# A decoder layer on one core: the second part of a long score row in the next score bank, and a different order of the operand splits

## The chip, the cores and the metric

The kernel runs on 1 core of one Trainium2 chip. Its time is the device time of one execution in microseconds; of three runs of the kernel before, the median is 2106.13 us (2105.40 to 2106.62). The profile is of one further execution, which took 2103.59 us. Engines are named as in the profile: PE is TensorE with its weight loads as PEld, DVE is VectorE, ACT is ScalarE, POOL is GpSimd, and SP is the engine that issues nearly all DMAs.

## The reference

One layer of a decoder with two kinds of attention side by side, over 2048 tokens of width 1024 with 16 learned meta tokens ahead of them, in fp32:

```python
xn = rms_norm(h, norm_gain[l])
proj = xn @ w_in[l]
sb_q, sb_k, sb_v, sw_q, sw_k, sw_v, sb_z, sw_z, g_sb, g_sw = jnp.split(proj, offsets, axis=-1)
o_sb = stick_breaking_attention(sb_q, sb_k, sb_v, valid)        # 8 heads of 64, over all earlier tokens
o_sw = sliding_window_sink_attention(rope(sw_q), rope(sw_k), sw_v, attn_sinks[l], valid)
y_sb = (o_sb * jax.nn.silu(sb_z)) @ w_branch_sb[l]
y_sw = (o_sw * jax.nn.silu(sw_z)) @ w_branch_swa[l]
merged = jax.nn.sigmoid(g_sb) * y_sb + jax.nn.sigmoid(g_sw) * y_sw
h = h + merged @ w_out[l]
```

Stick-breaking attention turns a row of scores z into weights through products of 1 - sigmoid(z) over the later keys:

```python
z = jnp.einsum('bqhd,bkhd->bhqk', q[:, q0:end], k[:, :end]) * scale
log_beta = jax.nn.log_sigmoid(z)
log_1m = jnp.where(mask, log_beta - z, 0.0)
rev = lax.cumsum(log_1m, axis=3, reverse=True)
suffix = jnp.concatenate([rev[..., 1:], jnp.zeros_like(rev[..., :1])], axis=-1)
w = jnp.where(mask, jnp.exp(log_beta + suffix), 0.0)
outs.append(jnp.einsum('bhqk,bkhd->bqhd', w, v[:, :end]))
```

## The kernel before

**Precision.** Matrix products run on fp32 operands that are split in two: a high part h (a cast on ACT) and a low part l = t - h (a subtraction on VectorE, or on GpSimd for some weights). A product is three matmuls, h·h, h·l and l·h. `put(hl, k, t)` (L1007) is such a split of 128 x 512 elements: the cast is L1008, the subtraction L1009.

**Order.** The tokens are reversed and cut into four groups of 512; the first half of the kernel works on groups 2 and 3 (`ga`, `gb` in the code), the second half on groups 0 and 1. In each half follow one another: projections woven with the sliding-window attention, projections woven with the stick-breaking attention (`stick`), and in the first half the last gates, in plain form and then by a scheme with seven products in place of eight (`combined`, `gate_pairs`). At the end of the kernel come the output products (`finish`). TensorE's instructions run in the order in which the program writes them (a manual schedule of PE over the whole kernel). For ACT, VectorE, GpSimd and SP a planner sets the order from a simulated timeline, except in blocks with a manual schedule of their own, which keep the written order among their instructions; others can be put between them.

**PSUM.** The eight banks (128 x 512 fp32) belong to four tags of two each: g for projections, z for scores, t for transposes, o for outputs. A tile of a tag gets a bank of the two that the planner finds free, and its first writer waits until the readers of the tile before are done.

**Stick-breaking attention (`stick`).** `weave` lets the projections, main, and the attention, side, take turns on TensorE. For each head h and group g a row step (n, j) takes the queries of block j against 512 keys. `row` (L896) writes the scores with two matmuls (L915; the two halves of the split q), applies a sigmoid on ACT (L918) and runs a scan on VectorE (L923 with the mask, L925 without) that carries on the product from the row before. The last row of a group (`end`) with four key blocks also has the 16 meta keys, 528 columns, more than a bank holds. Such a row comes once for each head and group, 32 times in all, and is done in two parts:

```python
pieces = [("z", 0, w)]
if end and nb == 4:
    pieces = [("z", 0, w // 2), ("o", w // 2, w // 2 + NM)]
    w += NM
banks = [ps(tag) for tag, _, _ in pieces]
```

`lt` row steps later (6 in the first half, 5 in the second) `turn` transposes blocks of the scanned rows on TensorE (L944) into a t bank and splits them (L126 on ACT, L127 on VectorE). `turn_meta` (L951) transposes the meta columns into an o bank (L954) and copies them to `wm` in four parts, by turns on ACT and VectorE (L958). `values` (L960) sums the products of the turned weights with differences of v in an o bank that a head and group holds from its first to its last values (L970); after the last ones, those with `wm`, ACT evicts the bank in four instructions with a bias (L976), and DMAs write it out. So three kinds of tiles share the two o banks in `stick`: the sums of `values`, the turned meta columns, and the second part of the long row.

**The scheme with seven products.** `first_sums` (L1022) makes four differences `firsts` = xh+xl of group gb less those of ga, in the ring of four tiles `xs` (`ring_x`), and three of the four differences `thirds` between halves of gb, in three tiles `tt` (`short`), before `stick` starts. `combined` (L1027) makes four operands of these: t2 and t4 in its generator `steps`, one k of four at each call, t3 from the thirds, and t1 from the firsts. t1 is written over the first half of `xh[gb]`, `xl[gb]` (L1031), which the plain gates still read. In `steps` the generator splits the three thirds into t3 after its last step, then makes the fourth with `step_back` (three VectorE operations, L1017 to L1019) in two more short tiles and splits it. `last` splits the firsts into t1. After the two plain gates the program calls

```python
drain(sums_x[4])
sums_x[5]()
```

that is the rest of `steps`, then `last`, in a manual schedule of VectorE and ACT. `gate_pairs` then runs the products (L1117, matmuls L1121 to L1123) in this order for the first pair: a11·b11, a12·b21, s2·t2, s4·b22, a22·t4, s1·t1, s3·t3, with banks g, z, t in turn; VectorE adds them (L1127) and so frees the banks. `pair_weights` (L1062) loads and splits the weights of a pair (L115, L119) and makes their sums (L1072 to L1088). `sums_ahead` (L1093) loads x for the next half into the `xs` ring, which the firsts hold until t1 is split, and squares it on ACT (L1101).

Of the kernel before, what the change touches and what calls it, by code (L numbers as in the profile page):

```python
# [20 lines left out]
NM = 16  # L21
# [22 lines left out]
def f32(ap):  # L44
    return ap.bitcast(F32)
# [3 lines left out]
def tile_kernel(ctx, tc, x, xt, meta, metat, gain, w_in, w_sb, w_sw, w_out, sinks, fgain,  # L49
# [16 lines left out]
    def ps(tag):  # L66
        return pp.tile([P, 512], F32, tag=tag, name="ps_" + tag, bufs={"g": 2, "z": 2, "t": 2, "o": 2}[tag])
# [319 lines left out]
    def tmp(dt=F32, rows=P):  # L387
        return tp.tile([rows, GT], dt, tag="tmp", name="tmp", bufs=9)
# [461 lines left out]
    def stick(groups, bp):  # L850
# [17 lines left out]
        def load_kv(h, g):  # L868

            p, a = divmod(h, 2)  # L870
            r = slice(64 * a, 64 * a + 64)
            if h not in kt:
                kt[h] = bp.tile([P, KW], F32R, tag="k", name="kt", bufs=2)
            for c in range(g, 4):
                if (h, c) in vc:
                    continue
                c0 = (c - groups[0]) * GT
                cs = slice(c0, c0 + GT + (NM if c == 3 else 0))
                DMA(kt[h][0:64, cs], kd[p][c][0][r])
                DMA(kt[h][64:128, cs], kd[p][c][1][r])  # L880
                v = vc[h, c] = bp.tile([P, 4, P], F32R, tag="v", name="vc", bufs=5)
                DMA(v, vd[p][c][a])

        def load_q(h, g):
            p, a = divmod(h, 2)
            r = slice(64 * a, 64 * a + 64)
            q1 = bp.tile([P, GT], F32R, tag="q1", name="q1", bufs=2)
            q2 = bp.tile([P, GT], F32R, tag="q2", name="q2", bufs=2)
            for t in range(2):
                DMA(q1[64 * t:64 * t + 64], qd[p][g][t][r])  # L890
                DMA(q2[64 * t:64 * t + 64], qd[p][g][1 - t][r])
            return q1, q2
# [3 lines left out]
        def row(h, g, n, j):  # L896

            if n == j == 0:
                load_kv(h, g)
                state[h, g] = {"q": load_q(h, g), "last": {}}  # L900
            st = state[h, g]
            last = st["last"]
            b0 = 4 * (g + n) + j
            nb = min(4, NB - b0)
            end = b0 + nb == NB
            w = nb * P + (NM if end and nb < 4 else 0)
            k0 = (b0 - 4 * groups[0]) * P
            pieces = [("z", 0, w)]
            if end and nb == 4:
                pieces = [("z", 0, w // 2), ("o", w // 2, w // 2 + NM)]  # L910
                w += NM
            banks = [ps(tag) for tag, _, _ in pieces]
            for t, qt in enumerate(st["q"]):
                for z, (_, c, m) in zip(banks, pieces):
                    T.matmul(z[:, :m], lhsT=qt[:, j * P:(j + 1) * P], rhs=kt[h][:, k0 + c:k0 + c + m], start=t == 0, stop=t == 1)  # L915
            r = bp.tile([P, RW], F32, tag="row", name="row", bufs=12)
            for z, (_, c, m) in zip(banks, pieces):
                A.activation(r[:, c:c + m], z[:, :m], AF.Sigmoid, scale=-1.0)  # L918
            if n == 0 and mask is None:
                G.affine_select(out=r[:, :P], in_=r[:, :P], pattern=[[1, P]], compare_op=ALU.is_ge,  # L920
                                fill=1.0, base=-1, channel_multiplier=-1)
            if n == 0 and mask is not None:
                V.tensor_tensor_scan(r[:, :w], r[:, :w], mask[:, :w], 1.0, op0=ALU.mult, op1=ALU.max)  # L923
            else:
                V.tensor_tensor_scan(r[:, :w], r[:, :w], r[:, :w], last[j] if n else 1.0, op0=ALU.mult, op1=ALU.min)  # L925
            last[j] = r[:, w - 1:w]
            rows_of[h, g, n, j] = r
            if end:
                if j == 0:
                    st["mr"] = bp.tile([P, 4, NM], F32, tag="mr", name="mr", bufs=2)  # L930
                G.tensor_copy(st["mr"][:, j], r[:, w - NM:w])  # L931
                if j == 3:
                    m = st["m"] = bp.tile([P, 4, 2, NM], F32R, tag="m", name="m", bufs=2)
                    A.copy(m[:, :, 0], st["mr"])
                    V.tensor_tensor(m[:, :, 1], st["mr"], f32(m[:, :, 0]), op=ALU.subtract)
# [48 lines left out]
        for s in range(n + lt + 3):  # L984
# [3 lines left out]
            t = s - lt  # L988
# [16 lines left out]
    HK = KT // 2  # L1005

    def put(hl, k, t):  # L1007
        A.copy(hl[0][:, k, :], t)  # L1008
        V.tensor_tensor(hl[1][:, k, :], t, f32(hl[0][:, k, :]), op=ALU.subtract)  # L1009

    def part(g, k):
        return f32(xh[g][:, k, :]), f32(xl[g][:, k, :])

    def step_back(t, k, g, k1, g1, e):

        (h0, l0), (h1, l1) = part(g, k), part(g1, k1)
        V.tensor_tensor(t, h0, h1, op=ALU.subtract)  # L1017
        V.tensor_tensor(e, l0, l1, op=ALU.subtract)
        V.tensor_tensor(t, t, e, op=ALU.add)  # L1019
        return t  # L1020
# [6 lines left out]
    def combined(ga, gb, pool, short, firsts, thirds):  # L1027

        t2, t3, t4 = [tuple(pool.tile([P, HK, GT], F32R, tag=f"{n}{s}", name=f"{n}{s}") for s in "hl")
                      for n in ("t2", "t3", "t4")]  # L1030
        t1 = (xh[gb], xl[gb])  # L1031

        def steps():
            rest = lambda: None
            for k, s in enumerate(firsts):
                (h21, l21), (h22, l22) = (part(g, k + HK) for g in (ga, gb))
                u, w = tmp(), tmp()
                V.tensor_tensor(u, h22, s, op=ALU.subtract)
                rest()
                V.tensor_tensor(u, u, l22, op=ALU.add)  # L1040
                A.copy(t2[0][:, k, :], u)
                V.tensor_tensor(w, h21, u, op=ALU.subtract)
                V.tensor_tensor(w, w, l21, op=ALU.add)
                A.copy(t4[0][:, k, :], w)
                V.tensor_tensor(t2[1][:, k, :], u, f32(t2[0][:, k, :]), op=ALU.subtract)

                def rest(k=k, w=w):
                    V.tensor_tensor(t4[1][:, k, :], w, f32(t4[0][:, k, :]), op=ALU.subtract)

                yield  # L1050
            rest()
            for k, t in enumerate(thirds):
                put(t3, k, t)
            for k in range(len(thirds), HK):
                put(t3, k, step_back(short(), k + HK, gb, k, gb, short()))

        def last():
            for k in range(HK):
                put(t1, k, firsts[k])
        return t1, t2, t3, t4, steps(), last  # L1060

    def pair_weights(c, d, pool, out, begin=False):  # L1062
# [282 lines left out]
    for half, groups in enumerate(halves):  # L1345
        gts = [lambda spec=spec: gate(*spec) for spec in specs[half]]
        with tc.tile_pool(name=f"swa{half}", bufs=1, side="left") as sp:
# [40 lines left out]
            else:  # L1388
                for mk, gs_ in ((sw_k, groups), (sw_v, groups), *((f, groups[:1]) for f in q[0])):
                    w, use, _ = mk()  # L1390
# [12 lines left out]
        if half == 0:  # L1403
            tt = mid.enter_context(tc.tile_pool(name="mid", bufs=1, side="left"))
            short = lambda: tt.tile([P, GT], F32, tag="tt", name="tt", bufs=3)
# [13 lines left out]
        if half == 0:  # L1419
            with tc.tile_pool(name="fast", bufs=1, side="left") as bp:  # L1420
                pairs = list(zip(specs[0][-FAST::2], specs[0][-FAST + 1::2]))
                sums_x = combined(*groups, bp, short, *early)
                byhand = ExitStack()
                byhand.enter_context(tc.manual_schedule(engines={mybir.EngineType.DVE}))
                with tc.manual_schedule(engines={mybir.EngineType.Activation}):
                    for n in range(PLAIN):
                        w, use, _ = plain[n]
                        for g in groups:
                            next(sums_x[4])
                            if n + 1 == PLAIN and g == groups[1]:  # L1430
                                drain(first_pair)
                            drain(lagged(col_tile(w, g, use)))
                        if n + 2 < PLAIN:
                            plain.append(gts[rest + n + 2]())
                        elif n + 2 == PLAIN:
                            nxt = []
                            first_pair = pair_weights(pairs[0][0][0], pairs[0][1][0], bp, nxt, True)
                            next(first_pair)
                    drain(sums_x[4])
                    sums_x[5]()  # L1440
                rs = tp.tile([P, 8], F32, tag="rs8", name="rs", bufs=1)
                rs0, rs1 = rs[:, :4], rs[:, 4:]
                gate_pairs(*groups, pairs, bp, sums_x, nxt, byhand.close, sums_ahead(halves[1], rs, short),
                           lambda: prep(halves[1][0], rs0))
                hsplit[0] = False
# [68 lines left out]
```

## Time and profile before

| | us |
|---|---|
| median of the three runs | 2106.13 |
| profiled execution | 2103.59 |
| its span | 2101.5 |
| PE busy | 2079.5 |
| DVE busy | 1474.4 |
| ACT busy | 1073.0 |
| POOL busy | 353.2 |

The span is the time from the first to the last instruction of the profiled execution; the 2.1 us around it belong to its time too. Busy times are sums of what each engine's instructions took. Matmuls overlap one another, and their ends are modelled; where the next matmul follows at once, its start lies before the end of the one ahead, so that the distance between starts is the surer measure. In the list of waits, a line names the engine and the line that waited, then what ended the wait, then the sum of the waits in us, their number and the longest. In the timeline each line has the start and the length in us, the engine, the line of the kernel, the operation, what it writes and reads, and in brackets the idle time of its engine just before and what ended it. "x4" means that four such instructions are drawn together.

The stick-breaking attention of the first half lies between 371 and 590 us of the span, the first pair of the seven-product scheme between 613 and 634 us, and the stick-breaking attention of the second half between 1110 and 1605 us.

### The profile page before, as it was taken

How to read it: one execution, taken by the hardware profiler on the slowest of the kernel's cores; microseconds unless marked ns; L12 is line 12 of the kernel's file. 1: busy time of each engine (PE TensorE's matmuls, PEld its weight loads, DVE VectorE, ACT ScalarE, POOL GpSimd, SP SyncE). 2: the span in 40 equal slices, each digit the busy share in tenths (PEclk: the TensorE clock that was granted, in tenths of full speed). 3: DMA queues.
4: the chain of work that ended last, by engine and by line, in shares of the span. 5: the costliest groups of instructions: out<-in, count | busy, mean ns of one | idle time of the engine just before them, and what ended most of it. 6: DMA issues, size and time to landing. Idle time of an engine off the chain costs nothing.

```text
span 2101.5 us, 31090 instructions
## 1 busy us (share of the span) xinstructions
PE 2079.5 (99%) x10591; PEld 1745.5 (83%) x10591; DVE 1474.4 (70%) x2430; ACT 1073.0 (51%) x2586; POOL 353.2 (17%) x692
## 2 busy tenths in 40 slices
PE   9999999999999999999999999999999999999998
PEld 7888888887888888888888888888888888888887
DVE  7898986877777554878747888878774446564553
ACT  6687774555656334877744555555554202320121
POOL 1234445322000000232310000000000243000000
PEclk9999999999999999999999999999999999999999
DMA  9855645766448674434445443443424996568432
GB/s 338 318 196 183 204 158 190 235 184 200 147 141 320 235 259 155 153 143 169 149 164 164 126 131 121 121 125 97 126 91 149 357 325 205 193 224 306 158 100 90
DMA packets 170094, 391.48 MB, mean 186 GB/s; under 512 B 23728, under 2 KB 28208, under 8 KB 169936
## 3 DMA queue, kind: packets, MB, share of 16 engines
q1 hardware_dynamic: 169648, 389.23, 55.2%
q8 instruction: 84, 1.38, 0.3%
q14 instruction: 74, 0.61, 0.1%
q10 hardware_dynamic: 288, 0.27, 0.0%
HBM read 241.68 MB, written 145.18 MB: 184 GB/s over the span
## 4 chain that ended last, share of the span: by engine, by line
PE 91%; DVE 3%; ACT 2%; DMA 2%; issue 1%; POOL 1%; SPq 0%; ACTq 0%; DVEq 0%; POOLq 0%
PE ps_g L461 39%; PE ps_o L970 6%; PE ps_z L915 5%; PE ps_t L944 5%; PE ps_z L756 3%; PE ps_o L812 2%; PE ps_z L461 2%; PE ps_g L258 1%; PE ps_g L259 1%; PE ps_g L260 1%; PE ps_z L258 1%; PE ps_z L259 1%; PE ps_z L260 1%; PE ps_t L258 1%; PE ps_t L259 1%; PE ps_t L260 1%
## 5 line engine op out<-in xcount | busy, mean ns | idle before, releaser
L461 PE MATMUL ps_g<-xh,wh 128*128 128x512 f32 x1296 | 529.3, 408 | 1.0 <-DVE tmp L677 0.6
L461 PE MATMUL ps_g<-xl,wh 128*128 128x512 f32 x1296 | 507.7, 392 | 0.5 <-DVE xl L1193 0.4
L461 PE MATMUL ps_g<-xh,wl 128*128 128x512 f32 x1296 | 507.6, 392 | 0.0
L925 DVE TENSOR_TENSOR_SCAN row<-row 128x512 f32<-128x512 f32 (+4 forms) x256 | 292.0, 1141 | 80.6 <-ACT row L918 45.5
L461 PEld LDWEIGHTS ps_g<-xh,wl 128*128 128x128 f32 x1296 | 243.4, 188 | 54.3 <-DVE wl L1241 0.4
L461 PEld LDWEIGHTS ps_g<-xh,wh 128*128 128x128 f32 x1296 | 244.2, 188 | 40.3 <-ACT xh L1192 1.3
L461 PEld LDWEIGHTS ps_g<-xl,wh 128*128 128x128 f32 x1296 | 244.7, 189 | 38.5 <-DVE xl L1193 1.6
L918 ACT ACTIVATE row<-ps_z 128x512 f32<-128x512 f32 (+2 forms) x320 | 165.5, 518 | 175.0 <-PE ps_z L915 170.3
L126 ACT ACTIVATE wth<-ps_t 128x512 fp32r<-128x512 f32 (+1 forms) x320 | 171.5, 536 | 67.1 <-PE ps_t L944 64.0
L127 DVE SCALAR_TENSOR_TENSOR wtl<-ps_t,wth 128x512 fp32r<-128x512 f32 (+1 forms) x320 | 189.7, 593 | 22.2 <-ACT wth L126 20.6
L915 PE MATMUL ps_z<-kt,q 128*128 128x512 f32 (+4 forms) x640 | 179.0, 354 | 0.0
L944 PE MATMUL ps_t<-ident,row 128*128 128x128 f32 x1088 | 171.0, 272 | 1.3 <-DVE wtl L127 1.3
L944 PEld LDWEIGHTS ps_t<-ident,row 128*128 128x128 f32 x1088 | 135.3, 140 | 34.1 <-DVE wtl L127 1.9
L915 PEld LDWEIGHTS ps_z<-kt,q 128*128 128x128 f32 x640 | 117.6, 188 | 22.3 <-ACT row L918 0.3
L970 PE MATMUL ps_o<-wth,vc 128*128 128x512 f32 (+1 forms) x320 | 131.8, 412 | 1.1 <-ACT tmp L976 1.1
L970 PE MATMUL ps_o<-wtl,vc 128*128 128x512 f32 (+1 forms) x320 | 116.3, 364 | 0.0
L764 ACT ACTIVATE sc<-sc,nm 128x129 f32<-128x129 f32 x256 | 100.0, 393 | 30.0 <-DVE nm L762 29.0
L931 POOL COPY mr<-row 128x16 f32<-128x16 f32 x128 | 27.9, 220 | 452.6 <-DVE row L925 410.4
L612 ACT ACTIVATE tmp<-ps_g 128x512 f32<-128x512 f32 x84 | 50.3, 599 | 86.6 <-PE ps_g L461 80.1
L117 POOL TENSOR_SCALAR wh<-raw 128x1024 fp32r<-128x1024 f32 (+1 forms) x47 | 53.5, 1138 | 224.6 <-PE ps_g L461 103.9
L123 POOL TENSOR_TENSOR wl<-raw,wh 128x256 fp32r<-128x256 f32 x96 | 86.4, 928 | 2.0
L297 ACT CAST ringl<-gt 128x512 fp32r<-128x512 f32 x32 | 19.9, 622 | 128.6 <-DVE gt L295 127.7
(444 smaller groups left out, 4177.8 us busy)
## 6 DMA issues: line engine op xcount, KB each, us to landing
wh<-h_in_w_in SPq DMA_DIRECT2D x66, 512.0 KB, 3.9
wl<-l_in_w_in SPq DMA_DIRECT2D x66, 512.0 KB, 5.0
h_in_w_in<-wh SPq DMA_DIRECT2D x50, 512.0 KB, 3.5
l_in_w_in<-wl SPq DMA_DIRECT2D x50, 512.0 KB, 4.0
raw<-in_w_in SPq DMA_DIRECT2D x49, 512.0 KB, 5.2
q<-qd SPq DMA_DIRECT2D x128, 128.0 KB, 3.1
vc<-vd SPq DMA_DIRECT2D x48, 256.0 KB, 2.9
kd<-tmp SPq DMA_DIRECT2D x32, 256.0 KB, 3.4
```

The source lines that it names most:

```text
L123: G.tensor_tensor(l[:, c], src[:, c], f32(h[:, c]), op=ALU.subtract)
L126: A.activation(h, acc, AF.Copy, scale=scale)
L127: V.scalar_tensor_tensor(l, acc, scale, f32(h), op0=ALU.mult, op1=ALU.subtract)
L258: T.matmul(acc, lhsT=wh[:, k, :], rhs=h, start=k == 0, stop=False)
L259: T.matmul(acc, lhsT=wh[:, k, :], rhs=l, start=False, stop=False)
L461: T.matmul(acc, lhsT=a[:, k, :], rhs=b[:, k, :], start=k == i == 0, stop=k == KT - 1 and i == 2)
L764: A.activation(sc[:, hh, :], sc[:, hh, :], AF.Exp, bias=nm[:, hh:hh + 1], accum_out=den[:, hh:hh + 1])
L915: T.matmul(z[:, :m], lhsT=qt[:, j * P:(j + 1) * P], rhs=kt[h][:, k0 + c:k0 + c + m], start=t == 0, stop=t == 1)
L918: A.activation(r[:, c:c + m], z[:, :m], AF.Sigmoid, scale=-1.0)
L925: V.tensor_tensor_scan(r[:, :w], r[:, :w], r[:, :w], last[j] if n else 1.0, op0=ALU.mult, op1=ALU.min)
L944: T.transpose(tr[:, j * P:(j + 1) * P], rows_of[h, g, n - (j > i), j][:, k0:k0 + P], ident)
L970: T.matmul(o[:, :n], lhsT=v, rhs=r, start=first and r is wh, stop=last)
```

## The change

There are two edits. In `row` the second part of the long row takes a z bank, as the first part does. In `combined` the splits of the thirds move from the end of `steps` to the end of `last`, behind the splits of t1, and the fourth third is made at the start of `last` (it reads the part of gb that t1 overwrites), in tiles of the `tmp` ring of nine in place of short ones.

```diff
@@ row
             if end and nb == 4:
-                pieces = [("z", 0, w // 2), ("o", w // 2, w // 2 + NM)]
+                pieces = [("z", 0, w // 2), ("z", w // 2, w // 2 + NM)]
                 w += NM
@@ combined
                 yield
             rest()
-            for k, t in enumerate(thirds):
-                put(t3, k, t)
-            for k in range(len(thirds), HK):
-                put(t3, k, step_back(short(), k + HK, gb, k, gb, short()))
 
         def last():
+            more = [step_back(tmp(), k + HK, gb, k, gb, tmp()) for k in range(len(thirds), HK)]
             for k in range(HK):
                 put(t1, k, firsts[k])
+            for k, t in enumerate(thirds + more):
+                put(t3, k, t)
```

## The prediction

> **What bounds the kernel now.** I read the page first, then the list of waits, then the timeline at each place where TensorE waits.
>
> ```profile
> span 2101.5 us, 31090 instructions
> ...
> PE 2079.5 (99%) x10591; PEld 1745.5 (83%) x10591; DVE 1474.4 (70%) x2430; ACT 1073.0 (51%) x2586; POOL 353.2 (17%) x692
> ```
>
> TensorE is busy 2079.5 of 2101.5 us. Only the other 22.0 us, and slow starts hidden in busy time, can be won without taking matmuls away; the change takes none away. The list of waits (engine, tile and line; what ended the wait; us in total, times, longest) says where they are. These rows touch the change:
>
> ```profile
> PE ps_o L915 <- DVE wm L958: 4.7, 4, 1.6
> PE ps_o L915 <- ACT tmp L976: 2.6, 3, 1.1
> ...
> PE ps_o L970 <- ACT tmp L976: 1.1, 2, 0.6
> ...
> PE ps_t L1121 <- ACT xh L1008: 1.2, 1, 1.2
> PE ps_z L1121 <- DVE tmp L1127: 0.6, 1, 0.6
> ...
> PE ps_t L1122 <- DVE xl L1009: 0.3, 1, 0.3
> ```
>
> The second part of the long row (ps_o, L915) waits seven times, 7.3 us together, for a bank of the output ring. The first t1 product (L1121, L1122) waits 1.5 us for its operands. Both lie in the first half of the sequence: the seven between 409 and 574 us, the product at 628 us.
>
> **The row's second part: what it removes.** Here is the timeline (start, length, engine, instruction; the bracket is idle time of its engine and what ended it) at an undisturbed row, at the first of the seven and at the last.
>
> ```profile
> 391.87 0.28 PE L915 MATMUL ps_z<-kt,q 128*128 128x256 f32 x1
> 391.98 0.29 PE L915 MATMUL ps_o<-kt,q 128*128 128x272 f32 x1
> ...
> 409.25 0.28 PE L915 MATMUL ps_z<-kt,q 128*128 128x256 f32 x1
> 410.31 0.36 PE L915 MATMUL ps_o<-kt,q 128*128 128x272 f32 x1 [0.79 <-DVE wm L958]
> 410.88 0.40 ACT L918 ACTIVATE row<-ps_z 128x256 f32<-128x256 f32 x1
> 412.13 0.54 PE L915 MATMUL ps_z<-kt,q 128*128 128x400 f32 x2
> ...
> 572.12 0.28 PE L915 MATMUL ps_z<-kt,q 128*128 128x256 f32 x1
> 573.27 0.26 ACT L958 CAST wm<-ps_o 32x128 fp32r<-32x128 f32 x1 [1.83 <-DVE wm L958]
> 573.55 1.14 ACT L976 ACTIVATE tmp<-ps_o,vf 128x128 f32<-128x128 f32 x4
> 574.00 0.36 PE L915 MATMUL ps_o<-kt,q 128*128 128x272 f32 x1 [1.61 <-DVE wm L958]
> 574.57 0.40 ACT L918 ACTIVATE row<-ps_z 128x256 f32<-128x256 f32 x1
> 575.37 0.39 PE L970 MATMUL ps_o<-wth,vc 128*128 128x512 f32 x1
> 575.83 0.53 PE L915 MATMUL ps_z<-kt,q 128*128 128x400 f32 x2
> ```
>
> Undisturbed, the second part starts 0.11 us after the first, the pitch of 256 columns (so 0.23 us for 512). At 409.25 it starts 1.06 us after, at 572.12 1.88 us after: 0.95 and 1.77 us lost. At such a place one output bank still holds the finished output of the head (evicted by L976, 1.14 us), the other the turned meta columns (copied out by ACT and VectorE in turn, L958). By the same subtraction the seven lose 0.95, 1.29, 0.95, 1.65, 1.28, 0.60 and 1.77, together **8.5 us**. Counting starts gives more than the idle 7.3, because a matmul that follows directly starts before the end drawn for the one ahead. The Trainium skill's page "Perfetto Trace Analysis", section "Identifying the Most-Contended Engine", says that matmul busy time misleads because matmuls are pipelined; by idle time alone my terms would come to 9.9 instead of 12.1 us.
>
> The row also takes the bank that the next values want; twice that costs TensorE a wait in the middle of a head:
>
> ```profile
> 446.36 0.38 PE L944 MATMUL ps_t<-ident,row 128*128 128x128 f32 x2
> 447.34 0.50 PE L970 MATMUL ps_o<-wth,vc 128*128 128x512 f32 x1 [0.60 <-ACT tmp L976]
> ```
>
> Two transposes, 256 columns, take 0.11 us; here 0.98 us pass, so 0.87 us are lost for 0.60 us of idle time. For both (1.1 us idle) that makes 1.1 + 2 x 0.27 = **1.6 us**. With the row gone from the ring a bank that was emptied steps earlier is free, so I count all of it (bounds 0 and 1.6).
>
> **What it adds.** Matmuls (256 and 272 columns) and sigmoids stay; no DMA is added. The row now holds both score banks. So its second part waits for the sigmoid of the row before, the next row for sigmoid 1, the one after that for sigmoid 2. Behind a waiting score matmul stands everything on TensorE, and so the transposes, the values and the gate products. In all 32 places I compared the row's start with the end of the sigmoid before it: it has ended, in the closest three of the second half at the very moment (bounds 0 to 0.2 us each; I take 0.3 us for the three). The new wait of the next row has slack too; the tightest of the second half is
>
> ```profile
> 1185.65 0.38 ACT L918 ACTIVATE row<-ps_z 128x256 f32<-128x256 f32 x1
> 1186.60 0.52 PE L915 MATMUL ps_z<-kt,q 128*128 128x400 f32 x2
> ```
>
> sigmoid 1 ends at 1186.03, 0.57 us before. At the seven places the stall itself was the cover. Take it out at 572: the next row would come at 575.83 - 1.77 = 574.06, but sigmoid 1 ends at 574.97, behind L976; and the next values (575.37) would come at 573.60, while L976 ends at 574.69. So about 1.1 us stays. At 409 the next row would come at 411.18 and sigmoid 1 ends at 411.28. Done so for all seven, with the values in L976's bank, 2.5 us stays. Bounds: 0, if the planner, which sets ACT's order anew, puts the sigmoids ahead of L976; 4.1, if the values also get the bank of the slow meta copies wherever that is later. I take 2.5, since ACT's order in the trace is the nearest row. This edit: 8.5 + 1.6 - 2.5 - 0.3 = **7.3 us** (bounds 8.5 - 4.1 - 0.6 = 3.8, and 10.1).
>
> That the other engines follow a faster TensorE is read from the stretch of these rows (length, then busy time and count per engine):
>
> ```profile
> 380.00:590.00 210.00, 200.84 (x1120) 168.73 (x1119) 165.77 (x254) 125.52 (x327) 40.69 (x90) 1.00 0.57 177
> ```
>
> VectorE, the fullest, has 44 us to spare, ACT 84. Clock 1.00.
>
> **The order of the splits.** The timeline at the t1 product:
>
> ```profile
> 613.34 0.39 PE L461 MATMUL ps_g<-xh,wl 128*128 128x512 f32 x1
> ...
> 620.01 1.65 ACT L1008 CAST t3h<-tt 128x512 fp32r<-128x512 f32 x3
> 620.69 0.68 DVE L1048 TENSOR_TENSOR t4l<-tmp,t4h 128x512 fp32r<-128x512 f32 x1
> ...
> 624.30 2.35 DVE L119 TENSOR_TENSOR wl<-raw,wh 128x1024 fp32r<-128x1024 f32 x2
> ...
> 626.94 0.39 PE L1123 MATMUL ps_z<-t4h,wl 128*128 128x512 f32 x1
> 627.29 0.62 ACT L1008 CAST t3h<-tt 128x512 fp32r<-128x512 f32 x1 [1.92 <-DVE tt L1019]
> 627.81 2.18 ACT L1008 CAST xh<-xs 128x512 fp32r<-128x512 f32 x4
> 628.48 0.50 PE L1121 MATMUL ps_t<-xh,sh 128*128 128x512 f32 x1 [1.15 <-ACT xh L1008]
> 628.55 2.49 DVE L1009 TENSOR_TENSOR xl<-xs,xh 128x512 fp32r<-128x512 f32 x4
> 629.29 0.50 PE L1122 MATMUL ps_t<-xl,sh 128*128 128x512 f32 x1 [0.30 <-DVE xl L1009]
> 629.62 0.40 PE L1123 MATMUL ps_t<-xh,sl 128*128 128x512 f32 x1
> ```
>
> At 0.23 us a matmul the product would start at 627.17. It starts 1.31 us late, its second matmul another 0.58, its third 0.10: **2.0 us**. Its inputs xh, xl are written last, after four t3 splits, of which the fourth waits for its sum, which waits behind 2.35 us of weight splits. After the edit ACT can cast xh from 620.0 on (the last reader of the old xh is the matmul at 613.34): four end by 622.2. VectorE does the moved sum (three operations of 0.62) from 621.3 to 623.2, then xl in 2.49: 625.7, or 628.0 if the weight splits go first. The last is wanted at 627.17 + 3 x 0.68 + 0.23 = 629.4. The t3 splits then end by 630.5 at the latest, wanted from 630.1 (first, ready 0.6 us after xl) to 632.2 (last). So the whole 2.0 us goes. The sum uses two tmp tiles instead of two short ones: no instruction more; should the tiles come late, each operation costs 0.62 of that slack.
>
> What could take it back is the next wait of this stretch, in the chain of waits:
>
> ```profile
> 629.26 3.16 DMA xs<-in_x
> ...
> 649.14 6.43 DMA raw<-in_w_in
> ```
>
> xl frees the tiles into which SP loads x, and behind those loads in SP's queue come the weights of a later pair; their lateness is the 0.6 us at ps_z L1121. With xl 3 to 5 us earlier those loads start earlier too, ahead of a TensorE that gains 2.0 there. I cost it at nothing; bounds: a gain of 0.8 (that wait, by starts), or a loss of the whole 2.0 if the weights keep their time. Edit: **2.0** (0 to 2.8).
>
> **Sum.** 7.3 + 2.0 = 9.3 us of the profiled execution's 2103.59 (2101.5 of span and 2.1 around it), so 2094.3. It lay 2.5 below the median of the runs, 2106.13; against that the forecast is **2096.8**. Bounds of the two edits: 3.8 to 12.9 us, so 2093.2 to 2102.3.
>
> **Rivals.**
> *The waits only move* (chance 0.12): in each head the meta copies and L976 hold up the next values instead of the row, and sigmoid 1 the next row, until all 8.5 us are back. Gain 1.6 + 2.0 - 0.3 = 3.3: 2102.8. For it: at 572 1.1 of 1.77 stays. Against it: at 435 and 518 I find nothing that would.
> *Half of it* (0.12): the lower bound, 3.8, with the pair's weights late: 2102.3; or the second edit alone fails because the planner puts weight splits ahead of xl and the sums too, 2106.13 - 7.3 = 2098.8. I take 2100.5 for the middle.
> *Slower* (0.10): a row that fills the score ring leaves no bank in which the next row can run ahead; from then on ACT's order decides. In the second half nothing is won to pay for it. If ACT put L976 (1.14) and a copy of a turned tile (0.60) ahead of sigmoid 1 in all 16 places there, 1.74 against a mean slack of 1.1 us costs 16 x 0.64 = 10.2; with the seven stalls replaced by equal ones and 2.0 won, 2106.1 + 10.2 - 2.0 = 2114.3. It decides from the point where sigmoid 1 starts over 1.1 us later than now. The Trainium skill's "Perfetto Trace Analysis", section "Matmuls", says that independent matmul groups should rotate through different banks so that an evacuation overlaps the next group; by that the row should not take the ring's two. Against it:
>
> ```profile
> ACT row L918 <- PE ps_z L915: 170.3, 238, 1.2
> ```
>
> of 320 such sigmoids 238 found ACT waiting for the score itself: the ring is mostly emptied at once.
> *That the change doesn't do what it says* would be a planner that leaves t1 behind t3; ACT and VectorE have a written order there, so it is inside "half of it".
>
> **How the numbers follow.** Forecast 0.66, half of it 0.12, only moved 0.12, slower 0.10. A measurement here can tell about 0.2%, 4.2 us, so faster is below 2101.9: forecast and the half give 0.78 and "only moved" 0.12 of no change, slower 0.10. The range reaches from the sum of all bounds, 2093.2, less 1 us for places that the planner orders anew, to just past "only moved", 2103.5; the slower rival is left out.
>
> **What would show it.** Right: no wait of L915 in the list, but short ones of L915 or L970 on ps_z or ps_o at 409 to 574, 2 to 3 us together; xh and xl cast ahead of t3 and no wait of L1121 on ps_t; the stretch to the t1 product shorter by 9 us. Wrong: rows of "PE ps_z L915 <- ACT row L918" with over 5 us, above all past 1110 us, or a longer wait of L1121 for L1127.

## The result, and the profile after

| | before | after | |
|---|---|---|---|
| median of the runs taken side by side (4 each), us | 2105.77 | 2093.16 | ratio 0.9941 [0.9924, 0.9958] |
| their range, us | 2104.93 to 2106.62 | 2092.05 to 2094.89 | |
| profiled execution, us | 2103.59 | 2092.70 | |
| its span, us | 2101.5 | 2090.5 | -11.0 |

The changed kernel is 12.6 us faster by the medians and 11.0 by the spans. The two numbers differ because the profile of before is of a quick execution: in the three later sets of runs of that kernel (15, 20 and 9 of them) the lowest times were 2103.97, 2103.63 and 2103.73. The page of the changed kernel:

```profile
span 2090.5 us, 31069 instructions
...
PE 2077.5 (99%) x10591; PEld 1744.9 (83%) x10591; DVE 1473.2 (70%) x2430; ACT 1071.6 (51%) x2586; POOL 350.9 (17%) x692
```

The work is the same (10591 matmuls, busy times within 0.7%); what is missing is idle time, and it is 13.0 us now (2090.5 less 2077.5) where it was 22.0. The list of waits of the changed kernel (what waited, what ended it; us in total, times, longest), its rows that touch the change:

```profile
PE ps_o L970 <- DVE wm L958: 0.5, 2, 0.3
...
PE ps_z L915 <- ACT row L918: 0.3, 1, 0.3
```

The seven waits of the row's second part, the two of the values for L976 and all waits of the t1 product are gone. Three short ones at heads' ends are left in this list, 0.8 us. (In the changed kernel the product's matmuls are L1120 to L1122 and its additions L1126, one line less than before.) The stretch of the long rows, in the view by windows (length, then busy time and count of PE, PEld, DVE, ACT, POOL; clock, DMA share, GB/s):

```profile
380.00:590.00 210.00, 208.36 (x1158) 175.91 (x1157) 171.81 (x266) 129.13 (x337) 41.89 (x90) 1.00 0.58 179
```

In the same 210 us TensorE starts 38 matmuls more, and VectorE and ACT follow with 6.0 and 3.6 us more work each. The clock is 1.00 as before.

**The stages.** One instruction that both kernels have is taken at each border, and the times between their starts are compared. The timeline of before, then that of the changed kernel (start, length, engine, instruction, idle before it), at a long row, the first matmul of the product s4·b22, the first projection that waits for L677, the first matmul of `finish` (L333) and the last DMA:

```profile
382.77 0.36 PE L915 MATMUL ps_z<-kt,q 128*128 128x256 f32 x1
...
624.45 0.39 PE L1121 MATMUL ps_z<-t4h,wh 128*128 128x512 f32 x1
...
848.22 0.50 PE L461 MATMUL ps_g<-xh,wh 128*128 128x512 f32 x1 [0.62 <-DVE tmp L677]
...
1789.46 0.39 PE L333 MATMUL ps_t<-ringr,ringl 128*128 128x512 f32 x1
...
2098.14 0.35 ACTq L370 DMA_DIRECT2D out<-a  x1
```

```profile
382.73 0.49 PE L915 MATMUL ps_z<-kt,q 128*128 128x256 f32 x2
...
615.53 0.39 PE L1120 MATMUL ps_z<-t4h,wh 128*128 128x512 f32 x1
...
836.06 0.50 PE L461 MATMUL ps_g<-xh,wh 128*128 128x512 f32 x1 [0.61 <-DVE tmp L677]
...
1777.32 0.39 PE L333 MATMUL ps_t<-ringr,ringl 128*128 128x512 f32 x1
...
2087.16 0.35 ACTq L370 DMA_DIRECT2D out<-a  x1
```

For each kernel of this study, from the same five starts of its profile (us):

| kernel | row to product | product to projection | to `finish` | `finish` |
|---|---|---|---|---|
| before | 241.68 | 223.77 | 941.24 | 308.68 |
| after | 232.80 | 220.53 | 941.26 | 309.84 |
| after, second profile (e10) | 232.80 | 221.54 | 941.30 | 309.63 |
| e1, first edit only | 232.82 | 222.60 | 941.37 | 311.08 |
| e2, second edit only | 241.58 | 221.36 | 941.21 | 309.66 |
| e9 | 232.80 | 223.11 | 941.29 | 308.89 |
| e5 | 232.86 | 220.99 | 941.29 | 310.02 |
| e3 | 241.37 | 223.11 | 947.22 | 309.04 |
| e4 | 240.18 | 220.48 | 942.50 | 310.30 |
| e8 | 234.56 | 224.67 | 941.19 | 309.69 |
| e7, e11 | 230.63, 230.66 | 220.94, 220.82 | 941.19, 941.30 | 309.46, 309.38 |

The change wins 8.88 us in the first column and 3.24 in the second, nothing in the third, and gives 1.16 back in the last. The first column repeats within 0.1 us for all kernels that have the same code there, the third within 0.2; the second and the last vary by 1 to 2.4 us without an edit there, so a difference of that size in them proves nothing by one profile. Taken together, the twelve profiles say more of the second: with the fourth t3 split ahead of t1 (before, e1, e3, e8, e9) it is 222.60 to 224.67, with that split behind t1 (the other seven) 220.48 to 221.54, on average 2.5 us less.

### The profile page after: what moved, and what is told of

It is laid out like the page before. It is cut to its first block, busy times and chain, and to the rows that moved or that the text cites. A ratio compares the mean times of both kernels' runs of the same rounds, so it can differ in the third digit from the quotient of the medians.

```text
span 2090.5 us, 31069 instructions
## 1 busy us (share of the span) xinstructions
PE 2077.5 (99%) x10591; PEld 1744.9 (83%) x10591; DVE 1473.2 (70%) x2430; ACT 1071.6 (51%) x2586; POOL 350.9 (17%) x692
## 3 DMA queue, kind: packets, MB, share of 16 engines
HBM read 241.68 MB, written 145.18 MB: 185 GB/s over the span
## 4 chain that ended last, share of the span: by engine, by line
PE 93%; DVE 3%; ACT 2%; DMA 1%; issue 1%; POOL 0%; SPq 0%; DVEq 0%; ACTq 0%; POOLq 0%
PE ps_g L461 41%; PE ps_o L970 6%; PE ps_z L915 6%; PE ps_t L944 6%; PE ps_z L756 3%; PE ps_o L812 2%; PE ps_z L461 2%; PE ps_g L260 1%; PE ps_g L258 1%; PE ps_g L259 1%; PE ps_t L790 1%; PE ps_z L260 1%; PE ps_z L258 1%; PE ps_z L259 1%; PE ps_t L260 1%; PE ps_t L259 1%
## 5 line engine op out<-in xcount | busy, mean ns | idle before, releaser
L918 ACT ACTIVATE row<-ps_z 128x512 f32<-128x512 f32 (+4 forms) x352 | 175.0, 508 | 169.5 <-PE ps_z L915 165.6
L915 PE MATMUL ps_z<-kt,q 128*128 128x512 f32 (+4 forms) x704 | 183.6, 349 | 0.4 <-ACT row L918 0.3
L915 PEld LDWEIGHTS ps_z<-kt,q 128*128 128x128 f32 x704 | 124.8, 188 | 25.7 <-ACT row L918 2.7
L970 PE MATMUL ps_o<-wth,vc 128*128 128x512 f32 (+1 forms) x320 | 131.5, 411 | 0.5 <-DVE wm L958 0.5
L970 PE MATMUL ps_o<-wtl,vc 128*128 128x512 f32 (+1 forms) x320 | 116.3, 364 | 0.0
```

The costliest lines, as they stand in the source:

```text
L970: T.matmul(o[:, :n], lhsT=v, rhs=r, start=first and r is wh, stop=last)
```

## The experiments

**Each edit alone.** e1 has only the first line of the diff, e2 only the edit in `combined`.

> Only the first edit: the second part of the long row in a score bank; the splits stay in the old order. Theory (the two edits act in two places and add up): by starts of TensorE the first edit gives back 8.5 (row) + 1.6 (values) less the 1.4 that the changed kernel still loses at its heads' ends, so about 9 us: ratio 0.9957. The late start at the t1 product (2.0) and the wait of a later product for L1127 (0.6 idle, 0.8 by starts) are still there. Rival (the planner's new order of everything after 371 us, and not the banks, brings the gain): the seven waits are gone, but the time is not 8 to 10 us below before, or the losses at the products are gone too.

> Only the second edit: t1 split ahead of t3, the fourth sum in tmp tiles; the row keeps its second part in the output ring. Theory: the 2.0 us at the t1 product go, and with the tiles of x free earlier the 0.8 at the later product too: 2 to 3 us, ratio 0.9987; the seven waits of L915 on ps_o stay at about 7.3 us. Rival (the later product's wait has nothing to do with the freed tiles): 2.0 at most, that wait stays or grows.

Measured: e1 2095.48 us against 2105.72, ratio 0.9950 [0.9938, 0.9963], so -10.2. e2 2101.76 against 2105.72, ratio 0.9982 [0.9974, 0.9991], so -4.0. The edits add up: 14.2 against the 12.6 of both together, within what the medians scatter, and 10.0 and 2.5 against 12.1 in the first two columns. For e2 2 to 3 us were expected; the second column bears that out (2.41), while the medians give more, with an interval of 1.9 to 5.5. The list of waits of e1:

```profile
PE ps_t L1121 <- ACT xh L1008: 1.2, 1, 1.2
...
PE ps_o L970 <- DVE wm L958: 0.5, 2, 0.3
...
PE ps_z L915 <- ACT row L918: 0.3, 1, 0.3
...
PE ps_t L1122 <- DVE xl L1009: 0.3, 1, 0.3
```

The t1 product waits as it did before, and the row's waits are those of the changed kernel. But the wait "PE ps_z L1121 <- DVE tmp L1127" of before, which the prediction tied to the order of the splits, is absent as well, with that order unchanged. It comes and goes by itself: in the second profile of the changed kernel (e10, below) the list of waits has

```profile
PE ps_g L1120 <- DVE tmp L1126: 0.5, 1, 0.5
```

and in the first it has no such row.

**The third products' operands.** If the product was late because the x splits queue behind one t3 split that must wait for its sum, then the three splits whose operands are ready may go back ahead of t1 at no cost (e5, from the changed kernel):

```diff
@@ combined, steps
             rest()
+            for k, t in enumerate(thirds):
+                put(t3, k, t)
@@ last
-            for k, t in enumerate(thirds + more):
+            for k, t in enumerate(more, len(thirds)):
                 put(t3, k, t)
```

> The changed kernel, but the three thirds that are ready are split into t3 ahead of t1, as before the change; the fourth sum is in tmp tiles and its split comes behind t1. It tells apart what made the t1 product late. Theory A (the fourth sum, late behind the weight splits and in front of t1 on both engines, did it): the product starts at most 0.5 us late, the time is that of the changed kernel within 1 us. Theory B (all four t3 splits ahead of t1 did it): the product is 1.5 to 2 us late again and so is the time.

Measured: 2093.90 against 2105.72, ratio 0.9945 [0.9930, 0.9961], so -11.8; the second column is 220.99. In the timeline of e5 the product starts when TensorE comes to it:

```profile
610.88 1.65 ACT L1008 CAST t3h<-tt 128x512 fp32r<-128x512 f32 x3
...
612.43 1.66 ACT L1008 CAST xh<-xs 128x512 fp32r<-128x512 f32 x3
...
618.03 0.39 PE L1122 MATMUL ps_t<-xh,sh 128*128 128x512 f32 x1
```

So what mattered is not that t3 stood ahead of t1, but that one split in ACT's written order was not ready. The other possibility, that the short tiles made the fourth sum late, is e9: the first edit, and in the old order the sum in `tmp` tiles.

```diff
@@ combined, steps
-                put(t3, k, step_back(short(), k + HK, gb, k, gb, short()))
+                put(t3, k, step_back(tmp(), k + HK, gb, k, gb, tmp()))
```

> The row as in the changed kernel; the splits in the old order (all t3, then t1), but the fourth sum in two tmp tiles in place of short ones. It tells what let the weight splits in ahead of the fourth sum. Theory T (the sum had to wait for short tiles that the first t3 splits free, and the weight splits went in while it waited): the t1 product starts at most 0.6 us late. Theory O (the order, t1 behind four t3 splits): it is still 1.5 to 2 us late.

Measured: 2095.86 against 2106.18, ratio 0.9953 [0.9938, 0.9968], so -10.3, no more than e1. Its timeline:

```profile
616.41 2.36 DVE L119 TENSOR_TENSOR wl<-raw,wh 128x1024 fp32r<-128x1024 f32 x2
...
619.40 0.62 ACT L1008 CAST t3h<-tmp 128x512 fp32r<-128x512 f32 x1 [1.86 <-DVE tmp L1019]
...
620.59 0.51 PE L1121 MATMUL ps_t<-xh,sh 128*128 128x512 f32 x1 [1.16 <-ACT xh L1008]
```

ACT idles 1.86 us for the sum, which VectorE does after the weight splits, and the product waits 1.16 us as before. The ring of the tiles is not the cause; the order is.

**Why the row waited.** Three kinds of tiles share the output ring, and the change moves one of them. e3 leaves the row there and moves another, the turned meta columns, to the t ring (from before):

```diff
@@ turn_meta
-            tr = ps("o")
+            tr = ps("t")
```

> The kernel before, with one line changed: turn_meta transposes the meta columns into a t bank instead of an output bank. The row keeps its second part in the output ring. Theory (three kinds of tiles on two output banks is what makes the row wait, so any one of them moved away frees it): the waits of L915 on ps_o fall from 7.3 to under 1 us; some of it comes back as waits of the transposes L944 for their two banks, since a t bank is then held through four slow copies: between 2098 and 2105 us in all. Rival (the row waits for L976 whatever else is in the ring): the row's waits stay above 5 us.

Measured: 2109.80 against 2104.89, ratio 1.0021 [1.0012, 1.0031], so 4.9 us slower: the expected time is missed. In its list of waits no L915 waits any more, but the transposes do:

```profile
PE ps_t L944 <- DVE wtl L127: 2.9, 5, 0.8
PE ps_t L954 <- DVE wtl L127: 2.9, 3, 1.3
PE ps_o L970 <- ACT tmp L976: 2.1, 5, 0.9
```

The first column is 0.3 us shorter than that of before, and the third, where the row had not waited at all, is 6.0 longer. In the first column TensorE also had a slow stretch: between 386.0 and 388.5 us, behind waits of 1.31 and 0.76 us, the granted clock is 0.50, which by starts costs 1.3 us; the waits alone would have left the column 1.6 us shorter than that of before. Of the weight loads of the transposes between 1110 and 1620 us it has

```profile
PEld ps_t L944 <- DVE wtl L127: 10.3, 17, 1.1
```

where before has one such wait, of 1.0 us. The meta columns did block the row, but the bank that they hold for their slow copies is now missed by the transposes. Taking a tile out of a ring is free only if the ring that gets it has time.

How slow the copies are shows in the timeline of before at the first of the seven heads, for ACT and VectorE:

```profile
408.34 0.24 ACT L958 CAST wm<-ps_o 32x128 fp32r<-32x128 f32 x1
409.58 0.26 ACT L958 CAST wm<-ps_o 32x128 fp32r<-32x128 f32 x1 [1.00 <-DVE wm L958]
...
408.70 0.53 DVE L127 SCALAR_TENSOR_TENSOR wtl<-ps_t,wth 128x384 fp32r<-128x384 f32 x1
409.26 0.28 DVE L958 CAST wm<-ps_o 32x128 fp32r<-32x128 f32 x1
409.87 0.30 DVE L958 CAST wm<-ps_o 32x128 fp32r<-32x128 f32 x1 [0.32 <-ACT wm L958]
```

Four copies of 0.24 to 0.30 us last from 408.34 to 410.17, 1.83 us, since each starts only after the one before it has ended on the other engine, and VectorE has a split of another tile to do first. e8 leaves both edits away and gives all four copies to ACT:

```diff
@@ turn_meta
-                (V.tensor_copy if j % 2 else A.copy)(w[r, j * P:(j + 1) * P], tr[r, :P])
+                A.copy(w[r, j * P:(j + 1) * P], tr[r, :P])
```

> The kernel before with one line changed: the four copies of the turned meta columns all on ACT. The row keeps its second part in the output ring. It tells apart what holds the output bank: theory S (the slow copies by turns; with them on ACT the meta bank is free about 1 us sooner, ahead of the row): the 4.7 us of row waits that ended on VectorE's copies go, and most of the others, because the row can take the meta bank: 6 to 9 us less than before, L915 waits under 2 us. Theory N (two banks are too few for three kinds of tiles whatever the copies take): the row's waits stay above 4 us.

Measured: 2096.94 against 2106.18, ratio 0.9957 [0.9943, 0.9970], so -9.2, just past the 6 to 9 expected. The copies in its timeline, and the row in its list of waits:

```profile
408.16 1.05 ACT L958 CAST wm<-ps_o 32x128 fp32r<-32x128 f32 x4
```

```profile
PE ps_o L915 <- ACT wm L958: 0.7, 2, 0.3
```

1.05 us in place of 1.83, and the row's waits fall from 7.3 to 0.7 us with the row still in the output ring. The first column is 7.12 shorter, four fifths of what the first edit brings. So it is the slow copies, and not the number of tiles in the ring, that made up most of the row's waits.

**ACT as the next limit.** The prediction's slower rival was that ACT's order decides once the row fills the score ring. e4 tests how much slack there is: the changed kernel evicts the head's output twice with the same values, so L976 takes 2.3 in place of 1.14 us.

```diff
@@ values
-                for j in range(4):
+                for j in (*range(4), *range(4)):
```

> The changed kernel with the eviction of the head's output (L976, four ACT instructions, 1.14 us) done twice over, the same values written twice. It lengthens ACT's work ahead of sigmoid 1 at the end of each head and group. Theory (with the row in both score banks ACT's order is the limit: the next row waits for sigmoid 1 behind L976): new waits of L915 on ps_z for L918 and of L970 on ps_o, 4 to 8 us in the first half; at the second half's looser ends at most 3. In all 2097 to 2104. Rival (ACT is off the path, its queue has room): the time stays within 1 us of the changed kernel.

Measured: 2100.02 against 2104.89, ratio 0.9975 [0.9965, 0.9984], so -4.9, which is 7.7 us less won than by the changed kernel. Of the waits in its list:

```profile
PE ps_o L970 <- ACT tmp L976: 3.0, 2, 1.8
...
PE ps_z L915 <- ACT row L918: 0.6, 2, 0.3
```

The first column loses 7.38 us of the 8.88, and not all of that is waiting. In the view by windows the stretch right behind the longest wait (1.83 us) has

```profile
519.00:523.00 4.00, 4.00 (x12) 3.22 (x13) 1.61 (x4) 0.72 (x3) 0.20 (x1) 0.57 0.96 306
```

TensorE is busy throughout, but its granted clock is 0.57 on average: the 512-column matmuls start 0.43 us apart where they otherwise start 0.23 apart. By starts this costs 1.5 us, and 5.9 us are left for the waits. The profile is of the slowest of e4's ten executions, 2102.30 us. The third column loses 1.24: between 1110 and 1620 us the weight loads of e4 have the wait

```profile
PEld ps_z L915 <- ACT row L918: 1.4, 5, 0.4
```

which those of the changed kernel do not have at all; the three longest of the five (0.33 to 0.36 us, at 1242, 1426 and 1549) are at the rows that the prediction meant by the closest three. So ACT is the next limit at the heads' ends, with less room than one more L976 (1.14 us).

**Both together.** e7 is the changed kernel with the copies of e8; e10 repeats the changed kernel and e11 repeats e7 on another chip, beside each other.

> The changed kernel with all four copies of the turned meta columns (L958) on ACT instead of by turns on ACT and VectorE. Theory (what is left at the heads' ends, 1.4 us by starts, comes from ACT waiting 1.0 to 1.8 us in its queue for VectorE's copies, with L976 and sigmoid 1 behind): these waits go, L970 and L915 lose under 0.5 us in all, the time is 1 us lower at best, which the trace shows rather than the clock. Rival: ACT has 0.5 us more to do ahead of sigmoid 1, and the next row waits longer than now, 1 to 3 us in all.

> The changed kernel once more, unaltered, beside the next one on the same chip: 2092 to 2095, ratio 0.994.

> The changed kernel with all four meta copies on ACT, once more, for the difference from the changed kernel on one chip. By the earlier traces it reaches the same late products 2 us sooner: 2 to 3 us below the changed kernel, ratio 0.993. If the earlier difference was the chip's or the planner's chance, it is within 1 us of it.

Measured: e7 2090.07 against 2104.89, ratio 0.9928 [0.9915, 0.9940], so -14.8. e10 2092.66 and e11 2090.87 against 2106.18, ratios 0.9938 [0.9926, 0.9951] and 0.9928 [0.9916, 0.9941]. On one chip e11 lies 1.8 us below the changed kernel; the times do not overlap (2090.00 to 2091.84 and 2092.20 to 2094.24), the intervals of the ratios do. The profiles agree: 2.17 and 2.14 us less in the first column, and no wait of L915 or L970 in their lists. The waits went as expected, but the size was missed: e7 had been given 1 us at best, because only the 1.4 us of the three listed waits were counted as left (2.0 are, see below), and e11, with 2 to 3 us expected, stays just under that by the medians (1.8). This is the fastest version found.

## Why the prediction was right, and where its terms were off

**The sum** was 9.3 us and 2096.8; measured were 12.6 by the medians, 11.0 by the spans. The measured 2093.16 lies at the very end of the sum of all bounds (2093.2) and is inside the range only by the 1 us added for places that the planner orders anew: that it fell inside is in part luck. What was off was off to the same side, too small a gain. The mechanism of both edits held: each works alone, in its own stage, by the waits that the prediction named, and e5 and e9 bear out what made the product late.

**First edit: 7.3 forecast, 8.88 measured.** The starts of the same matmuls in both kernels show that 8.5 and 1.6 are gone, as forecast. Mis-sized was what stays at the heads' ends: 2.5 forecast, 2.0 measured by starts. Of these, 1.4 are the three listed waits (0.44 at 488 us, 0.48 and 0.48 at 565). The other three, 0.23 at 411, 0.12 at 445 and 0.21 at 463, are in no list, because they lie under the end drawn for the matmul ahead. The timeline of the changed kernel at the first and the last of the seven heads:

```profile
409.40 0.26 ACT L958 CAST wm<-ps_o 32x128 fp32r<-32x128 f32 x1 [1.00 <-DVE wm L958]
409.68 1.14 ACT L976 ACTIVATE tmp<-ps_o,vf 128x128 f32<-128x128 f32 x4
410.38 0.48 PE L970 MATMUL ps_o<-wth,vc 128*128 128x512 f32 x1
410.69 0.40 PE L970 MATMUL ps_o<-wtl,vc 128*128 128x512 f32 x1
410.70 0.69 ACT L918 ACTIVATE row<-ps_z 128x256 f32<-128x256 f32 x2
411.15 0.63 PE L915 MATMUL ps_z<-kt,q 128*128 128x400 f32 x2
...
565.37 1.14 ACT L976 ACTIVATE tmp<-ps_o,vf 128x128 f32<-128x128 f32 x4
565.83 0.47 PE L970 MATMUL ps_o<-wth,vc 128*128 128x512 f32 x1 [0.32 <-DVE wm L958]
566.39 0.69 ACT L918 ACTIVATE row<-ps_z 128x256 f32<-128x256 f32 x2
566.84 0.63 PE L915 MATMUL ps_z<-kt,q 128*128 128x400 f32 x2 [0.31 <-ACT row L918]
```

ACT's order is the one that the prediction assumed. The step that failed is "with the values in L976's bank": at 410.38 they start while L976 still reads its bank (to 410.82), so they have the bank of the meta columns. The planner's choice goes by its simulated timeline: at four of the seven heads they have the bank of the meta columns, at three L976's. With that choice at each head the prediction's own working gives 1.9 in place of 2.5, and the seven heads show 1.84. At the last head it made little difference: the two waits there are 0.96 us, against the 1.1 of the prediction. As it said, the next row waits for sigmoid 1 behind L976: at 411.15, at 566.84 and at three more places it starts 0.05 us after that sigmoid's end. The mis-sized term explains 0.5 of the 1.3 us between 7.6 (8.5 + 1.6 - 2.5) and 8.88. The other 0.7 stand in no term: six starts in before (at 392, 420, 502, 529, 548 and 555 us) are 0.08 to 0.24 us later than in the changed kernel. The 0.3 for the three closest rows of the second half was nothing (941.24 and 941.26); they wait only when ACT gets more to do, in e4.

The prediction weighed the rule of the Trainium skill's page "Perfetto Trace Analysis", section "Matmuls", by which independent matmul groups rotate through different banks, against this edit. The runs say which side of it counts here: a row that fills its ring cost nothing in the second half, where ACT emptied it in time, 1.0 us of waits of the next row in the first half, and more as soon as the work of L976 doubled.

**Second edit: 2.0 forecast, about 2 measured.** The timeline of the changed kernel at the t1 product:

```profile
611.10 1.65 ACT L1008 CAST xh<-xs 128x512 fp32r<-128x512 f32 x3
...
616.11 2.35 DVE L119 TENSOR_TENSOR wl<-raw,wh 128x1024 fp32r<-128x1024 f32 x2
...
616.90 1.66 ACT L1008 CAST t3h<-tt 128x512 fp32r<-128x512 f32 x3
...
618.25 0.39 PE L1120 MATMUL ps_t<-xh,sh 128*128 128x512 f32 x1
...
618.48 0.39 PE L1121 MATMUL ps_t<-xl,sh 128*128 128x512 f32 x1
...
620.97 0.39 PE L1120 MATMUL ps_g<-t3h,sh 128*128 128x512 f32 x1
```

The xh splits go ahead, the product starts 2.72 us after the first matmul of s4·b22 (618.25 less 615.53) where it was 4.03 (628.48 less 624.45), its second matmul follows by 0.23, and the third product's operands are in time although the weight splits stand between. The second column won 3.24; 1.17 of that came without this edit in e1, 0.66 in e9. What is left, 2.1 to 2.6, is the 2.0 within the scatter of that column; so are the 2.5 us between the averages of the two groups of profiles. The step that the runs do not bear out is a reason, not a term: xl freeing the xs tiles and so the later weights. It was costed at nothing; the wait that it was to explain comes and goes with the order unchanged.

**The rest.** `finish` took 1.16 us longer than in before's profile. It lay between 308.68 and 311.08 in all twelve profiles, with no edit there, and before's was the shortest; why it varies stays open. This, and the quick execution that the profile of before was, is why the sum by spans and that by medians lie on both sides of the two columns' 12.1.

**Rivals.** "The waits only move" fell: 2.0 of 8.5 us stay. "Slower" did not happen, but its mechanism is real, as e4 shows; it lacked the delay of sigmoid 1 by over 1.1 us that the prediction named as the point from which it decides. The rows past 1110 us do not wait at all.

## What to carry to other kernels

When a matmul waits for a bank, look at what the bank's holder does all that time before giving the matmul another ring: here four short copies alternated between two engines and took 1.83 us for 1.05 us of work, and putting them on one engine alone won 7.1 us where the other bank won 8.9. A ring that is to take one more tile must be tried by its own next user, in every stage that has the tile: the score ring had that room, the transposes' ring did not and the kernel got slower in a stage where nothing had waited. In an engine's fixed order, one item that is not ready delays all that are ready behind it; it is enough to move that item.

## What the runs showed that was not expected

Copies of one bank by turns on two engines did not overlap: over the whole kernel of before, the view of L958 (idle before its instructions, by what ended it) has

```profile
  DVE wm L958: 17.8, 19
  ACT wm L958: 6.8, 20
```

so the engines idled 24.6 us for each other's copies, 17.8 of it on ACT. The copies read different quarters of the bank's partitions. In the trace each of the two engines waits for a semaphore that the other's copy raises, so it is the program that asks for the wait; whether the chip needs it was not tried.

Where nothing is edited in them, stages repeat unequally: the stick-breaking stretches within 0.2 us, the last stage within 2.4 us.

Two long waits of TensorE were followed by a loss of their own. In e3 and e4 the granted clock fell to one half for 3.4 us, each time right behind a stretch in which TensorE had been busy half of the time (1.75 of 3.50 us from 382.0 in e3, 1.67 of 3.50 from 515.6 in e4). In before TensorE was busy 1.79 of 3.40 us from 571.0, and the clock stayed 1.00; so what sets the fall off is not shown.
